# Sums of the MLP's weight blocks by accumulating DMAs, with the last norm in steps between products

## The chip, the cores and the metric

The kernel runs on one core of one Trainium2 chip. A core has engines with instruction queues of their own: TensorE (PE in the profile; PEld is its loading of weights), VectorE (DVE), ScalarE (ACT), GpSimd (POOL) and SyncE (SP), which here only issues DMAs. Each engine takes its instructions in order and waits on semaphores for what others produce. The metric is the device time of one execution in microseconds (us); lower is better. Times given for a kernel are medians of several runs.

## The reference

One layer of a hybrid decoder over 2048 prompt tokens and 32 sample tokens (8 sequences of 4), model width 1024, all in fp32:

```
h = rmsnorm(x, g_mix); proj = h @ w_in            # split into LRU x, LRU gate, SSD z, SSD x/B/C, SSD dt
y_lru = rmsnorm(RG_LRU(conv(lru_x)) * gelu(lru_gate))
y_ssd = rmsnorm(SSD_scan(silu(conv(ssd_xbc)), dt) * silu(ssd_z))
x = x + concat(y_lru, y_ssd) @ w_out              # 2048 -> 1024
h = rmsnorm(x, g_mlp)
x = x + square(relu(h @ w_up)) @ w_down           # 1024 -> 4096 -> 1024
y = rmsnorm(x, g_final)
```

It returns y for both kinds of tokens and the new states of the convolutions, of the LRU and of the SSD.

## The kernel before

**Numbers.** Each fp32 operand is split into a high part rounded to the fast matmul type and a low part (the remainder). A product is three matmuls: high × high, low × high, high × low. For a weight block of a projection `load_w` loads it (`raw`, L210), ACT makes the high part (`wh`, L212) and DVE the remainder (`wl`, L214).

**First phase, 0 to about 1741 us of the profile.** The tokens go through in three parts (768, 640 prompt and 32 sample, 640), each with two token blocks of up to 384. A part runs: the input phase `x_phase` (loads tokens, transposes them, L341, and norms them), `group_front`, eight SSD pairs (`pair_front`, `pair_x`, `pair_mats`, `pair_back`), eight LRU steps (`lru_front`, `lru_back`), then the output projection `proj_add`. That adds three groups of 512 or 1024 rows of `w_out` to the residual tiles `P.X2`: kt = 8 in the middle of the pairs, kt = 12 (half of the SSD's output, operands `n1`) and kt = 0 (the LRU's output, operands `nl`, split by `nl_split` during the kt = 12 call). Each call goes over eight output blocks `o` of 128. kt = 0 was called once for each token block and so loaded and split its eight weight blocks twice. Behind each block stood the square sums, and `residual_out`, which norms the block, and stores the MLP's input to `mn_d` and the residual to `x2_d` in DRAM. The last block's `residual_out` stood behind the next part's `x_phase`.

**Weight blocks of the MLP.** The MLP multiplies 2 × 2 blocks with seven products instead of eight. For each pair of column halves it needs seven matrices made from four weight blocks (some of them sums), split high and low, in `up_d` and `dn_d` in DRAM. Making them is cut into 64 jobs that are strewn through the first phase: `tick` counts work in units (TP at an SSD pair's places, TL at an LRU step's, TO at an output block of the kt = 0 projection) and issues the next stage of the current job each time a unit is full. Before, a job has four stages: load (four DMAs into one tile `jt`, L1077), sums (four DVE adds of 128 × 256, L1082 to L1085, and ACT's rounding into `jh`, L1087), lower (store of `jh`, DVE's remainder in place, L1091) and store (L1094). `jt` and `jh` have one buffer each, so a job's load waits for the job before to be stored.

**Second phase, the MLP.** Three tiles of about 696 tokens, each as two halves of up to 348 columns. For each of eight `q` it runs `up` twice (seven products of 12 matmuls, L816; PSUM from `bank()`) and `down` (four `g`, seven products of six matmuls each). `front` makes the operands of the next tile during the last `q`. `final` is the last norm of the tile before: for each 128 columns it transposes eight blocks of the residual (L975) into two PSUM tiles `fx`, squares and sums on ACT, norms on DVE into `yt` (three buffers, L985) and stores. Before, it was called in one piece behind the two `up` of q = 0, with the loads of the new tile's residual `x2` behind it.

The instructions of every engine's queue are put in order by a scheduler from the dependencies and from the order in which the code is written; nothing is fixed by hand beyond that.

Of the kernel before, what the change touches and what calls it, by code (L numbers as in the profile page):

```python
# [8 lines left out]
F32 = mybir.dt.float32  # L9
# [13 lines left out]
FF = 4096  # L23
# [15 lines left out]
TP, TL, TO = 1.4, 1.6, 1.0  # L39
X2N = ("m", "y", "xdt", "xdd", "hT")  # L40
XTN = ("xdt", "xdd", "hT")
HS, HR = 2, 4
# [3 lines left out]
def hymba_step(ctx: ExitStack, tc: tile.TileContext,  # L46
# [251 lines left out]
    def x_phase(P, mid=None):  # L298
        P.xT = dr.tile([D, P.Lc], F32, name=f"xT{P.i}")
# [28 lines left out]
        early = {}  # L328
        for ti, (a, n, gi) in enumerate(tiles):
            o = P.tt[a][0]  # L330
# [83 lines left out]
    def proj_add(P, src, kt, tiles, bc, blocks=None, hooks={}, tick=None):  # L414

        blocks = range(len(P.blocks)) if blocks is None else blocks
        nk = KD if isinstance(tiles[0], list) else len(tiles)
        per = KD // nk
        for o in range(KD):
            if o in hooks:  # L420
                hooks[o]()
            if tick:
                tick(P, TO)
# [3 lines left out]
            for b in blocks:  # L427
# [362 lines left out]
    def mlp():  # L790
# [11 lines left out]
        def tmp(name):  # L802
            return mp.tile([128, MH], F32, tag="t", name=name, bufs=20)
# [22 lines left out]
        def operands(b, n, tag, bufs):  # L826
# [3 lines left out]
            V.tensor_sub(t1[:, :n], b12[:, :n], b11[:, :n])  # L830
            V.tensor_sub(t2[:, :n], b22[:, :n], t1[:, :n])
            V.tensor_sub(t3[:, :n], b22[:, :n], b12[:, :n])
# [3 lines left out]
        def front(c0, n):  # L836

            out = [[] for _ in range(7)]
            b = []

            def load():
                for k in range(4):
                    b.append([tmp("mb") for _ in range(4)])
                for i in (0, 1, 3, 2):
                    for k in range(4):
                        o, hf = 128 * (k + 4 * (i // 2)), c0 + (i % 2) * n
                        nc.sync.dma_start(b[k][i][:, :n], mn_d[o:o + 128, hf:hf + n])
# [4 lines left out]
            def sub(d, x, y):  # L852
                V.tensor_sub(d[:, :n], x[:, :n], y[:, :n])

            t1 = []

            def one():
                half(0, [x[0] for x in b])
                for x in b:
                    t1.append(tmp("t1"))  # L860
                    sub(t1[-1], x[1], x[0])

            def two():
                for x, t in zip(b, t1):
                    sub(x[0], x[3], t)
                half(1, [x[0] for x in b])
                half(2, t1)

            def three():
                for x in b:  # L870
                    sub(x[1], x[3], x[1])
                half(3, [x[1] for x in b])
                half(4, [x[2] for x in b])
# [413 lines left out]
```

## Time and profile before

| what | value |
|---|---|
| median of three runs | 3186.7 us (3176.54 to 3188.68) |
| profiled execution | 3186.77 us |
| its span in the trace | 3185.0 us |
| mean granted clock of TensorE | 0.949 of full speed |
| busy in the span | PE 92%, PEld 88%, DVE 69%, ACT 44%, POOL 5% |
| DMA | 721.55 MB, q1 (issued by SP) 70.8% of 16 engines' span, q0 (issued by POOL) 0.1% |

A row of a stage table has a stretch of time, its length, the busy us of each engine with its instructions in brackets, the clock that TensorE was granted, the share of the DMA engines and GB/s. A row of groups has the line, engine, operation, tiles, shape and count, then the busy time in all, the mean in ns, the idle time before it and what ended that. A row of waits has who waited for whom, the us in all, how often and the mean.

### The profile page before, as it was taken

The numbers are of one execution on the slowest core, as the hardware profiler recorded it, in microseconds if no ns is written. First come the engines' busy times: TensorE is split into PE (matmuls) and PEld (weight loads), VectorE is DVE, ScalarE is ACT, GpSimd is POOL, SyncE is SP. The second block draws the span as 40 slices with busy tenths as digits, with TensorE's granted clock in tenths as the row PEclk, the third lists the DMA queues.
The fourth block names the chain that finished last, engine by engine and source line by source line (L and its number), as shares of the span: only waits on it lengthen the run. The fifth ranks groups of instructions, "written<-read, shape, count | busy, mean of one in ns | idle before, by whom it ended". The sixth has DMA issues, their size and how long they took to land.

```text
span 3185.0 us, 49175 instructions
## 1 busy us (share of the span) xinstructions
PE 2922.6 (92%) x18150; PEld 2812.0 (88%) x18150; DVE 2207.3 (69%) x4423; ACT 1407.6 (44%) x2580; POOL 158.8 (5%) x270
## 2 busy tenths in 40 slices
PE   7999999899999878998986999999799998699996
PEld 6999998788989877998975899998699998699996
DVE  6888788787777977887886554547555557454546
ACT  5544785444358635545862332324222224222322
POOL 0000110010002100001200000000000000000000
PEclk9999999899999988999997999999899999799997
DMA  6576566866665586565757888888688887688884
GB/s 190 171 227 172 183 195 205 251 187 198 194 187 172 167 268 217 164 207 157 224 171 220 304 270 281 268 284 270 233 274 280 270 283 259 220 269 276 267 279 150
DMA packets 555344, 721.55 MB, mean 227 GB/s; under 512 B 40709, under 2 KB 435129, under 8 KB 555104
## 3 DMA queue, kind: packets, MB, share of 16 engines
q1 hardware_dynamic: 554880, 718.13, 70.8%
q8 instruction: 144, 2.36, 0.3%
q0 software_dynamic: 224, 0.27, 0.1%
q14 instruction: 96, 0.79, 0.1%
HBM read 554.01 MB, written 164.27 MB: 226 GB/s over the span
## 4 chain that ended last, share of the span: by engine, by line
PE 47%; DVE 5%; DMA 5%; ACT 2%; issue 1%; SPq 0%; DVEq 0%; POOL 0%; ACTq 0%
PE mb L816 39%; PE mm L227 2%; PE mm L225 2%; PE mm L226 2%; DMA out_dram<-yt 1%; DMA mb<-mn_d 1%; DMA m<-cum 1%; DMA mw<-up 1%; DVE wl L214 0%; DMA mw<-dn 0%; DMA raw<-in_w_out_dram 0%; DVE yt L985 0%; DVE jt L1091 0%; PE ax L704 0%; DMA dn<-jt 0%
## 5 line engine op out<-in xcount | busy, mean ns | idle before, releaser
L225 PE MATMUL mm<-xh,wh 128*128 128x384 f32 (+3 forms) x2160 | 715.8, 332 | 49.4 <-ACT wh L212 22.0
L227 PE MATMUL mm<-xh,wl 128*128 128x384 f32 (+3 forms) x2160 | 711.9, 331 | 13.4 <-DVE wl L214 13.3
L226 PE MATMUL mm<-xl,wh 128*128 128x384 f32 (+3 forms) x2160 | 710.0, 329 | 1.5 <-DVE xl L360 0.8
L816 PE MATMUL mb<-ahh,mw 128*128 128x346 f32 (+1 forms) x2688 | 659.6, 326 | 18.9 <-DVE nt L242 7.7
L816 PE MATMUL mb<-mhh,mw 128*128 128x346 f32 (+1 forms) x2688 | 650.8, 322 | 25.5 <-DMA mw<-up 25.5
L816 PEld LDWEIGHTS mb<-ahh,mw 128*128 128x128 f32 x2688 | 476.0, 192 | 25.7 <-DVE nt L242 8.7
L816 PEld LDWEIGHTS mb<-mhh,mw 128*128 128x128 f32 x2688 | 475.0, 191 | 26.4 <-issue 21.0
L225 PEld LDWEIGHTS mm<-xh,wh 128*128 128x128 f32 (+1 forms) x2160 | 411.5, 191 | 66.0 <-ACT wh L212 24.9
L816 PE MATMUL mb<-ahl,mw 128*128 128x346 f32 (+1 forms) x1344 | 436.1, 325 | 0.1
L816 PE MATMUL mb<-mhl,mw 128*128 128x346 f32 (+1 forms) x1344 | 436.1, 325 | 0.0
L227 PEld LDWEIGHTS mm<-xh,wl 128*128 128x128 f32 (+1 forms) x2160 | 410.9, 190 | 26.6 <-DVE wl L214 20.4
L226 PEld LDWEIGHTS mm<-xl,wh 128*128 128x128 f32 (+1 forms) x2160 | 411.6, 191 | 7.0 <-DVE xl L360 2.4
L924 DVE TENSOR_TENSOR x<-x,mb 128x346 f32<-128x346 f32 (+1 forms) x480 | 244.3, 514 | 151.5 <-PE mb L816 148.3
L212 ACT ACTIVATE wh<-raw 128x1024 fp32r<-128x1024 f32 (+1 forms) x183 | 190.4, 1042 | 202.6 <-PE mm L226 138.8
L816 PEld LDWEIGHTS mb<-ahl,mw 128*128 128x128 f32 x1344 | 257.9, 192 | 0.6 <-DVE ahl L823 0.6
L816 PEld LDWEIGHTS mb<-mhl,mw 128*128 128x128 f32 x1344 | 254.9, 190 | 0.0
L214 DVE TENSOR_TENSOR wl<-raw,wh 128x1024 fp32r<-128x1024 f32 (+1 forms) x183 | 220.4, 1205 | 43.9 <-ACT wh L212 42.4
L889 ACT ACTIVATE p<-mb 128x346 f32<-128x346 f32 (+1 forms) x48 | 21.8, 455 | 474.9 <-PE mb L816 474.9
L396 DVE SCALAR_TENSOR_TENSOR u<-xe,prm,u 128x768 f32<-128x768 f32 (+2 forms) x180 | 169.7, 943 | 12.6 <-ACT u L394 10.6
L910 ACT ACTIVATE c<-c 128x346 f32<-128x346 f32 (+1 forms) x144 | 71.2, 494 | 203.0 <-DVE c L899 122.9
L823 DVE TENSOR_TENSOR ahl<-c,ahh 128x346 fp32r<-128x346 f32 (+1 forms) x144 | 74.1, 515 | 120.7 <-ACT ahh L822 120.5
L1091 DVE TENSOR_TENSOR jt<-jt,jh 128x1792 fp32r<-128x1792 f32 x64 | 129.3, 2021 | 25.9 <-ACT jh L1087 25.6
(297 smaller groups left out, 4276.1 us busy)
## 6 DMA issues: line engine op xcount, KB each, us to landing
mw<-up SPq DMA_DIRECT2D x336, 512.0 KB
mw<-dn SPq DMA_DIRECT2D x288, 512.0 KB
raw<-in_w_in_dram SPq DMA_DIRECT2D x108, 512.0 KB
raw<-in_w_out_dram SPq DMA_DIRECT2D x72, 512.0 KB
up<-jh SPq DMA_DIRECT2D x32, 896.0 KB
up<-jt SPq DMA_DIRECT2D x32, 896.0 KB
dn<-jh SPq DMA_DIRECT2D x32, 896.0 KB
dn<-jt SPq DMA_DIRECT2D x32, 896.0 KB
```

The lines of the kernel that those rows point to most:

```text
L212: S.activation(h, raw, AF.Copy)
L214: V.tensor_tensor(out=lo, in0=raw, in1=h.bitcast(F32), op=ALU.subtract)
L225: T.matmul(ps[:m, :n], h[:, k, :m], xh[:, c0:c0 + n], start=k == 0, stop=False)
L226: T.matmul(ps[:m, :n], h[:, k, :m], xl[:, c0:c0 + n], start=False, stop=False)
L227: T.matmul(ps[:m, :n], lo[:, k, :m], xh[:, c0:c0 + n], start=False, stop=k == nk - 1)
L396: V.scalar_tensor_tensor(out=u[:, :W], in0=xe[:, k:k + W], scalar=pc(wn, k * nt + j), in1=u[:, :W], op0=ALU.mult, op1=ALU.add)
L816: T.matmul(ps[:, :n], w[:, wi, c], x[:, :n], start=start and k == 0 and i == 0, stop=k == nk - 1 and i == 2, skip_group_check=not start)
L823: V.tensor_sub(lo[:, :n], t[:, :n], h[:, :n].bitcast(F32))
L889: S.activation(p1[:, :n], x[:, :n], AF.Copy)
L910: S.activation(c[:, :n], c[:, :n], AF.Relu)
L924: V.tensor_add(c, c, ps[:, :n])
L1091: V.tensor_tensor(out=jt[j].bitcast(F32R), in0=jt[j], in1=jh[j].bitcast(F32), op=ALU.subtract)
```

## The change

Four pieces go together.

1. The sums of a job are made by DMAs that add to their target, issued by POOL from SBUF to SBUF (`job_add`). The load puts each of the blocks that are needed twice into two places of `jt` at once (source step 0; eight DMAs instead of four, 896 KB instead of 512 KB). As such a DMA can only add, the minus signs move to the other operand and to the places where the products are added up: additions there become subtractions and the reverse, in the same number. A job has seven stages, and TP, TL, TO go from 1.4, 1.6, 1.0 to 2.5, 3.0, 1.0; every `proj_add` ticks now.
2. The projections at a part's end: kt = 12 for o 0 to 3, kt = 0 for both token blocks at once, then kt = 12 for o 4 to 7. `x_phase` is a generator: its pieces for the next part stand at o = 5 of kt = 0 and ahead of each pair of kt = 12 blocks. `residual_out` of both blocks stands behind the next part's `group_front`, in the last part behind everything.
3. `final` gives a list of steps of 128 columns, which `up` takes one by one behind its products 0, 2, 4 and 6 (`FILL`) at q = 0. The last tile's steps use `bank()`. The loads of `x2` stand in `down` at q = 0, two for each `g`.
4. `front` loads 12 of the 16 blocks first and `b21` in its fourth step; the tag `t` has 16 buffers, not 20.

```
-TP, TL, TO = 1.4, 1.6, 1.0
+TP, TL, TO = 2.5, 3.0, 1.0
+FILL = (0, 2, 4, 6)
...
-        for i, at in ((0, (0, 4)), (1, (3, 6))):
+        for at, i, r in ((0, 0, 0), (2, 1, 0), (4, 0, 1), (6, 1, 1)):
             for k in range(2):
-                nc.sync.dma_start(t[:, at[k]].rearrange("p (k n) -> p k n", n=128),
-                                  dap(src, (r0 + dr_ * k) * ld + cols[i], [[ld, 128], [128 * ld, 2], [1, 128]]))
-    def job_sums(j):
-        V.tensor_add(t[:, 2], t[:, 3], t[:, 6])
-        V.tensor_sub(t[:, 3], t[:, 0], t[:, 3])
-        V.tensor_sub(t[:, 1], t[:, 2], t[:, 0])
-        V.tensor_sub(t[:, 5], t[:, 4], t[:, 1])
+                m = min(2, 7 - at)
+                nc.sync.dma_start(t[:, at:at + m, 128 * k:128 * k + 128],
+                                  dap(src, (r0 + dr_ * r + 128 * k) * ld + cols[i], [[ld, 128], [0, m], [1, 128]]))
+    def job_add(j, to, of):
+        nc.gpsimd.dma_start(jt[j][:, to], jt[j][:, of], accum_op=ALU.add)
+    def job_first(j):
+        job_add(j, 2, 6)
+        job_add(j, 3, 0)
+    def job_second(j):
+        job_add(j, 1, 2)
+    def job_third(j):
+        job_add(j, 5, 1)
+    def job_higher(j):
         h = jh[j] = wp.tile([128, 7, 256], F32R, tag="jh", name="jh", bufs=1)
-        S.activation(h, t, AF.Copy)
+        S.activation(h, jt[j], AF.Copy)
...
-stages = (job_load, job_sums, job_lower, job_store)
+stages = (job_load, job_first, job_second, job_third, job_higher, job_lower, job_store)
...
-            V.tensor_add(v[:, :n], p1[:, :n], y[:, :n])
+            V.tensor_sub(v[:, :n], p1[:, :n], y[:, :n])
...
+        proj_add(P, w_out, 12, n1, bc1, range(4), {o: (lambda o=o: hook(o)) for o in range(4)})
+        xn = iter(()) if P.last else x_phase(parts[P.i + 1])
...
-        for b in range(lastb + 1):
-            proj_add(P, w_out, 0, nl, bcl, [b], tick=tick)
-            sums(b)
-            if b < lastb:
-                residual_out(b)
-        carried_out(P)
-        if not P.last:
-            x_phase(parts[P.i + 1])
-        residual_out(lastb)
+        proj_add(P, w_out, 0, nl, bcl, hooks={5: lambda: next(xn, None)})
+        for o in (4, 6):
+            next(xn, None)
+            proj_add(P, w_out, 12, n1, bc1, range(o, o + 2))
+        for _ in xn:
+            pass
+        for b in range(lastb + 1):
+            sums(b)
+        carried_out(P)
...
-                act = [up(q, u, mh, n) for u in range(2)]
-                if prev:
-                    final(*prev)
+                act = [up(q, u, mh, n, fill) for u in range(2)]
```

What this moves is seen in the queues. On PE at the first tile change (`fx` are the transposes of `final`, `mb` the MLP's products) the end of the norm stands before as

```order
L816 MATMUL mb<-ahh,mw 128x346
L975 MATMUL fx<-ident,x_18056 128x128
L975 MATMUL fx<-ident,x_18058 128x128
L975 MATMUL fx<-ident,x_18060 128x128
L975 MATMUL fx<-ident,x_18062 128x128
L975 MATMUL fx<-ident,x_18064 128x128
```

with 32 such rows in a run, four steps of eight. After, the fourth step and what follows it reads

```order
L1000 MATMUL fx<-ident,x_18175 128x128
L822 MATMUL mb<-ahh,mw 128x346
L822 MATMUL mb<-ahl,mw 128x346
L822 MATMUL mb<-ahh,mw 128x346 x2
L822 MATMUL mb<-ahl,mw 128x346
L822 MATMUL mb<-ahh,mw 128x346 x2
```

and some 50 products stand there ahead of the next eight transposes; only the last two steps stand nearly side by side, with five products between them.

On POOL, in the LRU steps of the first part (`xe`, `halo`, `hl` and `u` belong to the LRU; `jt` is the job's tile), the queue before is

```order
L378 COPY xe<-halo 128x3
L770 TENSOR_TENSOR u<-a 128x768
L386 COPY halo<-xe 128x3
L781 COPY hl<-th 128x1
L378 COPY xe<-halo 128x3
```

and after

```order
L1102 DMA jt<-jt 128x256
L776 TENSOR_TENSOR u<-a 128x768
L1102 DMA jt<-jt 128x256 x2
L394 COPY halo<-xe 128x3
L1102 DMA jt<-jt 128x256
L787 COPY hl<-th 128x1
L386 COPY xe<-halo 128x3
```

so the LRU's small work on POOL now stands behind DMAs that wait for a load or for the DMA before.

On PE at the end of part 1 (`mm` with `xh` of 128 columns are projection products, `ax<-ident,xt` the transposes of the next part's tokens, `mm` of 16 columns the next part's first products) the order before is

```order
L227 MATMUL mm<-xh,wl 128x288
L1027 MATMUL ax<-ident,so 24x128 x4
L1027 MATMUL ax<-ident,soh 8x128 x8
L341 MATMUL ax<-ident,xt 128x128 x12
L287 MATMUL nx<-ident,rs 128x128 x3
L341 MATMUL ax<-ident,xt 128x128 x6
L225 MATMUL mm<-xh,wh 16x384
```

and after, where `nh` and `nl` are the operands of kt = 12,

```order
L229 MATMUL mm<-xh,wl 128x288
L349 MATMUL ax<-ident,xt 128x128 x11
L227 MATMUL mm<-nh,wh 128x384
L228 MATMUL mm<-nl,wh 128x384
L229 MATMUL mm<-nh,wl 128x384
L227 MATMUL mm<-nh,wh 128x384
```

so the transposes of the next part's first tokens stand ahead of projection products, and the carried states come behind.

More of the change, by code (lines that the diff above doesn't have):

```diff
@@ L426, in proj_add @@
             w = [t[:, :, 128 * (o % per):128 * (o % per) + 128] for t in ws]
-            for b in blocks:
+            for b in range(len(P.blocks)):
                 c0, n = P.blocks[b]
@@ L849, in half, with sub, loads @@
             def half(op, ts):
                 out[op].extend(halves(t, n, "mh", 56) for t in ts)
-            def sub(d, x, y):
-                V.tensor_sub(d[:, :n], x[:, :n], y[:, :n])
-            t1 = []
+            def sub(d, x, y, op=ALU.subtract):
+                for i in range(4):
+                    V.tensor_tensor(out=d[i][:, :n], in0=x[i][:, :n], in1=y[i][:, :n], op=op)
+            def loads():
+                load(b11, 0, c0)
+                load(b12, 0, c0 + n)
+                load(b22, 512, c0 + n)
@@ L857, in one @@
             def one():
[L858 to L861, printed above, removed]
+                half(0, b11)
+                sub(b11, b11, b12)
             def two():
[L864 to L867, printed above, removed]
+                t2.extend(tmp("t2") for _ in range(4))
+                sub(t2, b22, b11, ALU.add)
@@ L881, in front, with after, up @@
-            return out, [load, one, two, three, four]
-        def up(q, u, mh, n):
+                half(4, b21)
+                half(5, b22)
+                sub(b21, b21, t2)
+                half(6, b21)
+            return out, [loads, one, two, three, four]
+        def after(i, fill):
+            if fill and i in FILL:
+                fill.pop(0)()
+        def up(q, u, mh, n, fill=()):
             src = up_d[2 * q + u]
@@ L887, in up @@
             product(x, weights(src, 0, 512), mh[0], n, True)
+            after(0, fill)
             p1 = tmp("p1")
@@ L903, in up @@
             product(z, weights(src, 5, 512), mh[5], n, False)
+            after(5, fill)
             c12 = tmp("c12")
@@ L968, in final, with step @@
                     m = s1 - c0 - o
+                steps.append((o, m))
+                o += m
+            def step(o, m):
                 ss = sf.tile([128, 8], F32, tag="ssq", name="ssq")
@@ L992, in final @@
                                               yts[hf][lo - c0 - o:hi - c0 - o])
-                o += m
+            return [lambda a=a: step(*a) for a in steps]
         mh, steps = front(*MLP[0])
@@ L1016, in mlp @@
                     steps.pop(0)()
-                down(q, act, x2, us, n, steps)
-            prev = (c0, n, x2)
-        final(*prev)
+                down(q, act, x2, us, c0, n, steps)
+            fill = final(c0, n, x2, i + 1 == len(MLP))
+        for f in fill:
+            f()
     def rows_out(src, j0, nt, m, dst, ld):
@@ L1142, in hymba_step @@
         R0 = group_front(P, 0, lambda: decays(P))
+        if P.i:
+            residual()
         fr = pair_front(P, 0)
```

133 lines of the change are left out of this document (71 added, 62 removed).

## The prediction

> **What bounds the kernel now.** I read the page first: its totals, the tenths of granted clock, the queues. It puts TensorE (PE) at the top and leaves GpSimd (POOL) and its DMA queue all but empty.
>
> ```profile
> span 3185.0 us, 49175 instructions
> PE 2922.6 (92%) x18150; PEld 2812.0 (88%) x18150; DVE 2207.3 (69%) x4423; ACT 1407.6 (44%) x2580; POOL 158.8 (5%) x270
> ...
> q0 software_dynamic: 224, 0.27, 0.1%
> ```
>
> So time can only be had where PE stands still or runs at a lowered clock. A table by stage shows where (columns: stretch, its length, busy us of PE, PEld, DVE, ACT and POOL with counts, granted clock, DMA share, GB/s):
>
> ```profile
> 340.00:500.00 160.00, 152.41 (x859) 150.41 (x858) 134.36 (x173) 133.22 (x176) 29.71 (x29) 0.98 0.59 187
> 500.00:640.00 140.00, 124.53 (x671) 110.80 (x670) 109.90 (x232) 65.96 (x113) 3.33 (x6) 0.89 0.75 233
> 640.00:945.00 305.00, 292.89 (x1951) 268.32 (x1950) 242.38 (x504) 141.98 (x266) 22.78 (x72) 0.96 0.65 189
> ...
> 1090.00:1240.00 150.00, 119.14 (x677) 106.09 (x676) 112.28 (x250) 66.59 (x121) 0.50 (x3) 0.84 0.74 229
> ...
> 1640.00:1760.00 120.00, 80.75 (x468) 75.87 (x467) 83.83 (x174) 37.58 (x58) 2.78 (x1) 0.80 0.69 215
> sum 1720.00, PE 1572.52 PEld 1481.24 DVE 1391.33 ACT 963.89 POOL 156.20; mean PE 174.72 PEld 164.58 DVE 154.59 ACT 107.10 POOL 17.36
> ```
>
> Inside a part (third row: 305 us, the SSD pairs of part 1) PE has 12 us idle and a clock of 0.96. The three boundaries are the bad places: 500–640, 1090–1240 and 1640–1760. In each of them idle time is followed by a lowered clock, so an idle gap is paid more than once. Next the same table for the MLP's products alone (L816; first pair PE, second PEld) at a steady place, at the two tile changes and at the end:
>
> ```profile
> 1820.00:2160.00 340.00, 340.00 (x2137) 339.29 (x2136) 1.00 0.84 276
> 2220.00:2280.00 60.00, 29.67 (x168) 27.68 (x167) 0.74 0.60 198
> 2700.00:2760.00 60.00, 27.76 (x141) 25.76 (x140) 0.69 0.57 185
> ```
>
> The steady MLP is full: 340/2137 = 0.159 us per product. It has nothing to give except at the tile changes. There the transposes of the last norm (L975) wait for one another, and the timeline of PE shows by how much (start, length, work, and in brackets the idle time before it and its releaser):
>
> ```profile
> 2252.47 1.97 PE L975 MATMUL fx<-ident,x 128*128 128x128 f32 x8 [4.00 <-DVE yt L985]
> ...
> 2264.41 1.91 PE L975 MATMUL fx<-ident,x 128*56 128x128 f32 x8 [3.99 <-DVE yt L985]
> 2269.57 0.66 PE L816 MATMUL mb<-ahh,mw 128*128 128x346 f32 x1 [3.25 <-DVE nt L242]
> ```
>
> Each 128-column step costs 2 us of transposes and 4 us of waiting for DVE to empty the two PSUM banks.
>
> **The change part by part.**
>
> *Last norm in steps between products.* In 2220–2280 the products alone would need 168 × 0.159 = 26.7 us, the transposes take 42 × 0.157 = 6.6 us (the row below), so 60 − 26.7 − 6.6 = 26.7 us are lost; in 2700–2760 it is 60 − 141 × 0.159 − 6.6 = 31.0 us.
>
> ```profile
> 2220.00:2280.00 60.00, 9.45 (x42) 6.99 (x42) 0.74 0.60 198
> ```
>
> Together 57.7 us. Now four of the six steps are followed by a product or more of 12 matmuls (1.9 us each at 0.159; the order puts about 45 to 60 of them, 7 to 9 us, behind each), and 4 us of DVE work fit under that. Steps 4 and 5 stand almost side by side and keep one 4.0 us wait; the second wait (3.25 us, for the first operands of `down`) keeps its cause; the small work of the steps now lies between the DVE and ACT work that `up` needs. I leave 11 us lost per change: 57.7 − 22 = 36 gained. Ends: 57.7 if nothing stays, 10 if the evictions of `up` queue behind the six norm steps on DVE and PE waits 4 us at each of the 12 steps (57.7 − 48). The out DMAs of a step move behind up to 12 weight loads on SP's queue and hold `yt` longer; yt has three buffers for two per step, so the next step waits for those DMAs. That is in the 22. The x2 loads move from one run of eight into the four `g` of `down`; the steady stretch has a DMA share of 0.84, so they fit, at 0.
>
> *End of the kernel.* The last six steps have six banks now, but `yt` still has three buffers. The chain of waits there:
>
> ```profile
> 3174.65 0.76 DVE yt L985
> ...
> 3175.43 2.00 DMA out_dram<-yt
> ```
>
> A step's time passes through yt and its store, which the banks don't change: −2 us, between 0 and −6 (one step).
>
> *Order at a part's end.* Against the clock and fill of a quiet stretch (0.97, no idle), 500–640 loses 140 − 124.5 = 15.5 idle and 124.5 × (1 − 0.89/0.97) = 10.3 by clock, 26 us; 1090–1240 loses 30.9 + 16.0 = 47 us. Most of it lies in the next part's input phase, which PE waits for after its last projection product. In the new order that phase runs beside projection products of kt = 0 (o 5 to 7) and kt = 12 (o 4 to 7), and the residual's norm and stores go behind the next part's group_front. Two thirds of 26 + 47 is 48 gained; one third stays, since the square sums and carried_out still stand alone and the residual's DVE work meets the next part. Ends: all 73, and 0 if ACT and DVE, which do both the input phase and the weight splits, only change the order in which they are late. For the third boundary (39 idle, of which the next row shows 20.6) I take 0: there is no next part to overlap, the residual of both blocks now comes in one piece (up to +5), and four of 16 operand loads fewer stand ahead of the first weights (down to −8).
>
> ```profile
> PE mb L816 <- DMA mw<-up: 25.5, 3, 20.6
> ...
> PE mm L227 <- DVE wl L214: 16.9, 21, 1.7
> ...
> PE mm L225 <- DVE x L432: 11.6, 10, 2.3
> ```
>
> *DVE and ACT work taken away.* The sums of the weight blocks are four DVE instructions for each of 64 jobs, and the projections now load and split each kt = 0 weight block once for both token blocks: 24 splits fewer.
>
> ```profile
> L214 DVE TENSOR_TENSOR wl<-raw,wh 128x1024 fp32r<-128x1024 f32 (+1 forms) x183 | 220.4, 1205 | 43.9 <-ACT wh L212 42.4
> ...
> L1085 DVE TENSOR_TENSOR jt<-jt 128x256 f32<-128x256 f32 x64 | 29.8, 466 | 0.8
> ...
> L1083 DVE TENSOR_TENSOR jt<-jt 128x256 f32<-128x256 f32 x64 | 28.0, 437 | 1.0
> ...
> L1082 DVE TENSOR_TENSOR jt<-jt 128x256 f32<-128x256 f32 x64 | 27.2, 425 | 26.2 <-DMA jt<-in_w_up_dram 9.8 <-DMA jt<-in_w_down_dram 8.9 <-issue 7.3
> ...
> L1084 DVE TENSOR_TENSOR jt<-jt 128x256 f32<-128x256 f32 x64 | 26.7, 417 | 0.0
> ```
>
> That is 29.8 + 28.0 + 27.2 + 26.7 = 111.7 us of DVE plus 24 × 1.205 = 29 us of splits. DVE isn't the bound, so it counts only where PE waited for DVE: 16.9 + 11.6 = 28.5 us in the rows above. 141 of the 1391 us of DVE in this phase (the sum row of the table by stage) is a tenth; since DVE's work comes in bursts I take a quarter, −8 us (0 to −28). The signs moved into subtractions cost 0: the same count of DVE operations.
>
> *Sums by accumulating DMAs.* A job now is eight loads, then three dependent links of DMAs of 128 KB on POOL's queue (2+=6 beside 3+=0; 1+=2; 5+=1), then rounding, remainder, two stores. There is one `jt` and one `jh`, so a job's round is a chain; the chain of waits shows one round before:
>
> ```profile
> 1513.61 2.04 DVE jt L1091
> ...
> 1515.66 5.19 DMA dn<-jt
> ...
> 1521.29 0.49 SPq L1077
> ...
> 1521.83 0.46 SPq L1077
> ...
> 1522.34 3.01 DMA jt<-in_w_up_dram
> ...
> 1525.48 0.43 DVE jt L1082
> ...
> 1528.12 1.70 ACT jh L1087
> ```
>
> After: 2.04 + 5.19 + 8 issues × 0.475 + 3.01 + 1.70 + 0.4 of handoffs = 16.1 us, plus 3 L for the links. No accumulating DMA stands in this trace. The nearest rows are POOL's few DMAs:
>
> ```profile
> cum<-cT POOLq DMA_DIRECT2D x1, 48.0 KB, 2.5
> ...
> cum<-cT POOLq DMA_DIRECT2D x1, 40.0 KB, 1.9
> ...
> ecum<-eT POOLq DMA_DIRECT2D x1, 40.0 KB, 6.4
> ```
>
> Ends of L: 1.9 and 6.4 us. I take 2.8: the first row, 2.5, and 0.3 for a transfer some three times as large. So a round is 16.1 + 8.4 = 24.5 us (21.8 to 35.3). By the Trainium skill (DMA: Bandwidth & Descriptors, section on the anatomy of one DMA on the gpsimd path) such a DMA is estimated at 2.0 us + bytes/436e3; 128 KB gives 2.3 us, a round of 23.0 us, and the +20 below would be 0, 3093 us in all. What is free for a round:
>
> ```profile
> sum 1681.00, ACT 106.80; mean ACT 11.87
> ```
>
> That is the rounding instruction (L1087) over 60–1741 us, 64 times: 26.3 us for each job, 25.4 once the boundaries have given 56. A round of 24.5 just fits on the mean, but stages fall at fixed places in the program, and a late link holds the POOL queue (the LRU's copies behind it), then ACT's rounding, then SP's stores with the weight loads behind. I put +20 on it, between 0 (L = 1.9) and 60 + 64 × 35.3 − 1683 = +636 (L = 6.4). The added traffic (about 384 KB more loads for each job, 512 KB of accumulates, less 24 weight blocks of 512 KB) is some 46 MB over 1700 us, 27 GB/s on 190 to 230: at 0, since the DMA share there is 0.6 to 0.75.
>
> **Sum:** −36 − 2 − 48 − 8 + 20 = −74 us. The profiled execution took 3186.77 us (span 3185.0 and 1.8 around it), the median of the three runs is 3186.7, so nothing is to be corrected: 3113 us.
>
> **Rivals.**
> 1. *The chain of jobs becomes the bound of the first 1740 us.* Point of decision: without the +20 the gain is 94, of which 58 lie before the MLP, so the phase ends at 1683; 60 + 64 C = 1683 + 94 gives C = 26.8, L = 3.6. At L = 4.5, C = 29.6 and the end is at 1954, +271: 3187 − 94 + 271 = 3364. For it: one POOL DMA took 6.4, and 190–230 GB/s of other traffic go past. Against: the other rows are 1.9 to 2.5. Nearer the point of decision, L = 4.1, it is 3187 − 94 + (60 + 64 × 28.4 − 1683) = 3288.
> 2. *The boundaries don't close:* ACT and DVE are late as before, 48 becomes about 10: 3151. For it: PE waits there for ACT's and DVE's pieces of the input norm, both of which now also serve products. Against: DVE is at 110 of 140 and ACT at 66 of 140 in that stretch.
> 3. *The norm between the products stalls them* (the 10 end above, evictions and SP's queue): 3113 + 26 = 3139.
> 4. *POOL is held by DVE.* POOL's own small copies show it: the same copy of 128x3 takes from 0.18 to 2.9 us.
>
> ```profile
> L378 POOL COPY xe<-halo x60: 176/186/2885, 36.7 to 1592.9; 128x3 f32<-128x3 f32 x60
> L386 POOL COPY halo<-xe x60: 185/527/1995, 53.8 to 1599.0; 128x3 f32<-128x3 f32 x60
> ```
>
> If each link pays the usual excess (0.527 − 0.185 = 0.34 us), C is 25.5, and the jobs cost some 10 us more than forecast, 3123; if each pays the worst (2.7 us), C is 32.6, and 60 + 64 × 32.6 − 1683 = +463. I hold the first for the likely form, with a quarter of the chance at a middle of 1 us (C = 27.5, +137, 3230). The Trainium skill (SBUF — State Buffer, the box on DVE blocking DMAs) says that a DMA issued from GpSimd can't write its descriptors while DVE holds their shared port in a fast copy, and looks blocked: it speaks against this change, and the spread of the copies agrees that DVE can hold POOL, but no row here shows a DMA held.
>
> **How the numbers follow.** Forecast 3113: 0.46. Rival 1: 0.20. Rival 2: 0.14. Rival 3: 0.12. Rival 4: 0.08. A measurement of this kernel can tell 0.5% from no change, 16 us: below 3171 or above 3203. Faster: 0.45 of the forecast, 0.11 of rival 2, 0.10 of rival 3, 0.05 of rival 4, 0.71. Slower: 0.17 of rival 1, 0.02 of rival 4, 0.01 of rival 2, 0.20. Same: the remaining 0.09. The range goes from 3060 (the good ends of half the terms: 3113 − 20 − 25 − 8) to 3250, inside rival 1 (L = 3.6 gives 3187, L = 3.9 gives 60 + 64 × 27.8 − 1683 = +156, 3249); 0.06 lies below and 0.12 above. The forecast's own range is 3075 to 3150.
>
> **What would show it.** Right: q0 carries some 33 MB, and an accumulate lands in about 3 us; a round of the job chain is 24 to 25 us; the MLP begins near 1705; the two tile changes have some 11 us lost each, and no run of eight transposes waits 4 us except one; the clock at 500–640 and 1090–1240 goes above 0.92. Wrong: an accumulate of 4 us or more, ACT's rounding or POOL's copies waiting for it, SP's issues waiting for ACT; idle stretches at the boundaries as before with other releasers; products released by the evictions of `up` at the tile changes. The prediction fails above all on L, and next on the share of the boundary that closes.

## The result, and the profile after

| | before | changed |
|---|---|---|
| median | 3184.8 us (4 runs, 3176.5 to 3188.7) | 3377.1 us (4 runs, 3374.4 to 3381.7) |
| ratio to before | 1 | 1.061 (95% interval 1.058 to 1.063) |
| span of the profiled execution | 3185.0 us | 3373.8 us |
| first product of the MLP | 1756.8 us | 1986.4 us |
| from there to the end | 1428.2 us | 1387.4 us |

The forecast was 3113 us; the change is 6.1% slower. The MLP became 41 us shorter and the first phase 230 us longer. The time of run 6 below leaves out one execution that took 5932.7 us. The first phase is read from the start of the MLP's first product (rows of before and of the changed kernel; ns shortest, median, longest, then first and last start in us):

```profile
L816 PE MATMUL mb<-mhh,mw x2688: 317/322/629, 1756.8 to 3119.2; 128*128 128x346 f32 x128, 128*128 128x348 f32 x64
```

```profile
L822 PE MATMUL mb<-mhh,mw x2688: 315/322/628, 1986.4 to 3307.8; 128*128 128x346 f32 x128, 128*128 128x348 f32 x64
```

The page of the changed kernel, against the rows shown of before:

```profile
span 3373.8 us, 50181 instructions
PE 2964.2 (88%) x18150; PEld 2849.1 (84%) x18150; DVE 2096.8 (62%) x4143; ACT 1383.1 (41%) x2556; POOL 363.0 (11%) x526
...
q0 software_dynamic: 37088, 33.85, 6.8%
...
jt<-jt POOLq DMA_DIRECT2D x256, 128.0 KB, 3.4
```

DVE is busy for 110 us less, and q0 carries the 33 MB of accumulates. Yet PE's share fell: 1946 us of first phase for the same work as before in 1716 (the first row is of before, up to its first MLP product, the second of the changed kernel; columns as in the table by stage).

```profile
40.00:1756.00 1716.00, 1569.34 (x9860) 1478.03 (x9858) 1389.61 (x2536) 963.89 (x1551) 156.20 (x258) 0.95 0.65 197
```

```profile
40.00:1986.00 1946.00, 1624.36 (x9858) 1529.71 (x9857) 1278.99 (x2251) 939.00 (x1525) 360.39 (x514) 0.90 0.72 197
```

PE's idle time grew from 147 to 322 us, and its granted clock fell from 0.95 to 0.90, with 55 us more busy time for the same products. The waits (who waited for whom, us in all, times, longest) name the jobs:

```profile
POOL jt L1102 <- DMA jt<-jt: 357.0, 112, 7.2
...
DVE jt L1120 <- ACT jh L1116: 265.0, 53, 12.9
...
ACT jh L1116 <- DMA jt<-jt: 195.1, 32, 18.3
...
PE mm L227 <- ACT xe L391: 54.5, 16, 7.3
PE mm L227 <- DVE x L438: 53.4, 15, 11.0
```

The rows of before that belong to the third, second and fourth of these (the fifth, L432, stands in the prediction):

```profile
ACT jh L1087 <- DVE jt L1085: 68.4, 24, 7.1
...
DVE jt L1091 <- ACT jh L1087: 25.6, 29, 3.1
...
PE mm L225 <- ACT xe L383: 11.5, 8, 3.7
```

Read from the top: POOL waits for one accumulating DMA before it can issue the next; ACT's rounding (L1116) waits for the last; DVE's remainder (L1120) waits for ACT, ten times as long as before; and PE waits 54.5 and 53.4 us, before 11.5 and 11.6, for other work of ACT and DVE, which take their queues in order. A round of one job can be followed in the timeline, here on POOL:

```profile
1130.03 0.88 POOL L1102 DMA_DIRECT2D jt<-jt  x1 [2.46 <-issue]
1131.22 0.86 POOL L1102 DMA_DIRECT2D jt<-jt  x1 [0.31 <-issue]
...
1137.51 0.86 POOL L1102 DMA_DIRECT2D jt<-jt  x1 [4.46 <-DMA jt<-jt]
...
1140.49 0.86 POOL L1102 DMA_DIRECT2D jt<-jt  x1 [0.87 <-DMA jt<-jt]
```

and on ACT, DVE and SP behind it:

```profile
1145.17 1.70 ACT L1116 ACTIVATE jh<-jt 128x1792 fp32r<-128x1792 f32 x1 [5.58 <-issue]
...
1146.90 2.03 DVE L1120 TENSOR_TENSOR jt<-jt,jh 128x1792 fp32r<-128x1792 f32 x1 [6.06 <-ACT jh L1116]
...
1148.96 0.56 SPq L1123 DMA_DIRECT2D up<-jt  x1
1154.06 3.92 SPq L1098 DMA_DIRECT2D jt<-in_w_down_dram  x8
```

From the first accumulating DMA to the rounding 15 us pass. SP holds the next load until the store has landed, as there is one `jt`; it waited for that in 52 rounds (in before in 38):

```profile
SPq L1098 <- DMA up<-jt: 88.2, 28, 6.9
...
SPq L1098 <- DMA dn<-jt: 63.8, 24, 5.6
```

Over the 63 rounds the starts in the timeline give these medians (us): rounding to remainder 1.7, remainder to store 2.1, store to the next load 5.7, the eight loads' issues 4.0, to the first DMA 0.9, to the second 1.6, to the third 4.9, to the fourth 3.2, to the next rounding 2.9. Their sum is 26.9 us (27.0 from the rounded figures), of which 12.5 us stand for the links. This is a middle and no floor: 8 of the 63 rounds were shorter, the shortest 24.5 us. The rounds themselves, from the starts of the rounding, look so:

| rounds (us) | mean | quartiles | shortest |
|---|---|---|---|
| before | 26.1 | 19.1, 22.7, 29.9 | 16.0 |
| changed | 30.1 | 27.8, 29.5, 31.3 | 24.5 |

The ends of the two series of 64 roundings are these rows (first and last start):

```profile
L1087 ACT ACTIVATE jh<-jt x64: 1680/1697/1721, 51.6 to 1695.1; 128x1792 fp32r<-128x1792 f32 x64
```

```profile
L1116 ACT ACTIVATE jh<-jt x64: 1687/1701/1711, 64.3 to 1959.6; 128x1792 fp32r<-128x1792 f32 x64
```

Before, half of the rounds took less than 23 us, and three over 50. In the changed kernel there are hardly any short rounds, and the last rounding stands 27 us ahead of the MLP instead of 62. The theory to be tested is the *theory of the rounds*: each round lasts the longer of the chain and of what the program puts between two jobs. If the n rounds of a kernel whose chain doesn't bind are filled up to a chain of C, the first phase grows by the sum of (C − round) over the shorter ones. The rivals: the accumulates' *traffic*; and a *queue theory* or *theory of standing*, in which the waits of POOL, ACT and DVE at a job's stages cost by themselves, however much room a round has.

The MLP did what was forecast. Its products alone, in 140 us around each tile change, before and changed:

```profile
2160.00:2300.00 140.00, 101.81 (x601) 98.02 (x600) 0.87 0.74 249
...
2640.00:2780.00 140.00, 99.19 (x554) 95.65 (x554) 0.83 0.70 236
```

```profile
2390.00:2530.00 140.00, 117.21 (x692) 111.70 (x691) 0.95 0.83 276
...
2870.00:3010.00 140.00, 123.00 (x734) 118.38 (x734) 0.96 0.84 278
```

At 0.159 us for a product, 91 and 180 more of them in the same time are 14.5 and 28.6 us, 43 in all.

### The profile page after: what moved, and what is told of

It reads as the page before. It is cut to its first block, busy times and chain, and to the rows that moved or that the text cites. A ratio compares the mean times of both kernels' runs of the same rounds, so it can differ in the third digit from the quotient of the medians.

```text
span 3373.8 us, 50181 instructions
## 1 busy us (share of the span) xinstructions
PE 2964.2 (88%) x18150; PEld 2849.1 (84%) x18150; DVE 2096.8 (62%) x4143; ACT 1383.1 (41%) x2556; POOL 363.0 (11%) x526
## 5 line engine op out<-in xcount | busy, mean ns | idle before, releaser
L227 PE MATMUL mm<-xh,wh 128*128 128x384 f32 (+3 forms) x2160 | 726.2, 337 | 95.2 <-ACT xe L391 54.5
L228 PE MATMUL mm<-xl,wh 128*128 128x384 f32 (+3 forms) x2160 | 719.7, 334 | 1.1 <-DVE xl L481 1.0
L227 PEld LDWEIGHTS mm<-xh,wh 128*128 128x128 f32 (+1 forms) x2160 | 420.5, 195 | 114.7 <-ACT xe L391 60.1
L229 PEld LDWEIGHTS mm<-xh,wl 128*128 128x128 f32 (+1 forms) x2160 | 418.5, 194 | 20.1 <-DVE wl L216 13.8
L228 PEld LDWEIGHTS mm<-xl,wh 128*128 128x128 f32 (+1 forms) x2160 | 419.6, 194 | 7.1 <-DVE xl L481 2.2
L1102 POOL DMA_DIRECT2D jt<-jt x256 | 221.5, 867 | 1025.6 <-DMA jt<-jt 357.0
L1120 DVE TENSOR_TENSOR jt<-jt,jh 128x1792 fp32r<-128x1792 f32 x64 | 129.5, 2024 | 267.1 <-ACT jh L1116 265.0
L214 ACT ACTIVATE wh<-raw 128x1024 fp32r<-128x1024 f32 (+1 forms) x159 | 165.5, 1042 | 220.0 <-PE mm L228 205.4
L1116 ACT ACTIVATE jh<-jt 128x1792 fp32r<-128x1792 f32 x64 | 108.8, 1701 | 340.3 <-DMA jt<-jt 195.1
L216 DVE TENSOR_TENSOR wl<-raw,wh 128x1024 fp32r<-128x1024 f32 (+1 forms) x159 | 191.1, 1202 | 33.0 <-ACT wh L214 32.0
```

Source lines behind the costliest of these rows:

```text
L214: S.activation(h, raw, AF.Copy)
L216: V.tensor_tensor(out=lo, in0=raw, in1=h.bitcast(F32), op=ALU.subtract)
L227: T.matmul(ps[:m, :n], h[:, k, :m], xh[:, c0:c0 + n], start=k == 0, stop=False)
L228: T.matmul(ps[:m, :n], h[:, k, :m], xl[:, c0:c0 + n], start=False, stop=False)
L229: T.matmul(ps[:m, :n], lo[:, k, :m], xh[:, c0:c0 + n], start=False, stop=k == nk - 1)
L1102: nc.gpsimd.dma_start(jt[j][:, to], jt[j][:, of], accum_op=ALU.add)
```

## The experiments

Each is an edit of the changed kernel unless it says otherwise; times are medians, each against the kernel before on the same chip (medians 3183 to 3197 us).

**1. Sums by DVE at the same places.**

```
-        nc.gpsimd.dma_start(jt[j][:, to], jt[j][:, of], accum_op=ALU.add)
+        V.tensor_add(jt[j][:, to], jt[j][:, to], jt[j][:, of])
```

> The changed kernel with one thing undone: the four sums of a job are DVE adds again (four of 128 x 256), at the same places of the program, with the same eight loads, seven stages and ticks; the projections' order and the norm's steps stay. Chain theory (the round of one job, load to load, paces the first phase; in the changed kernel it takes 30.1 us on the mean, of which 14.1 us lie in the links of the accumulating DMAs): the links fall to about 4 x 0.45 + handoffs = 3 us, the round to some 19 us, below what the program offers, and the phase is as long as its other work: the MLP starts near 1700 to 1730 us, the time is 3090 to 3120 us. Queue theory (the stages' places in the in-order queues cost, whoever adds): half of the 230 us stays, 3200 to 3260 us. Traffic theory (the added DMA bytes cost): 256 DMAs gone, the larger loads stay; 3110 to 3150 us.

Measured: 3130.8 us, ratio 0.982 (0.980 to 0.984); the MLP begins at 1739.1. Who adds is worth 247 us of first phase (1986.4 − 1739.1). 3131 lies just above the chain's range and inside the traffic's, so this run alone does not tell the two apart; runs 2 and 3 bear on that, and run 7 shows where the excess is.

**2. One link instead of three, same DMAs.**

```
-        job_add(j, 1, 2)
+        job_add(j, 1, 4)
...
-        job_add(j, 5, 1)
+        job_add(j, 5, 4)
```

> The changed kernel with the same 256 accumulating DMAs and bytes, but the second and third read a block that the load has brought (1+=4 and 5+=4 in place of 1+=2 and 5+=1), so none waits for another: one link in a row instead of three (the sums are other ones). Chain theory: 5.0 + 3.9 us of waiting between links become about 1.3 us of issue each, the round falls from 30.1 to some 24 us, the time to 3110 to 3170 us. Traffic theory: nothing changes, 3360 to 3390 us. Queue theory: ACT and DVE wait at the same places but shorter, 3200 to 3300 us.

Measured: 3264.3 us, ratio 1.024 (1.020 to 1.027); MLP at 1870.3. Bytes and count being the same, 116 us came back, so traffic alone is not the cause. But 131 us over run 1 stayed, more than the chain alone would give, and this run doesn't say what they are. The four DMAs in flight together took longer each (median 4.4 us to landing, not 3.4).

**3. One link more.**

```
         job_add(j, 5, 1)
+        job_add(j, 5, 1)
```

> The changed kernel with the last accumulating DMA done three times in place of once... in fact twice: job_third issues 5+=1 two times (another sum), so a job has four dependent links instead of three and 320 DMAs instead of 256. Chain theory: one more link of 3.4 to 5 us in each of 64 rounds, +220 to +320 us, 3600 to 3700 us, the MLP's length unchanged at 1387 us. Traffic theory: a quarter more of the accumulates' traffic, +50 us at most, 3430 us. Queue theory: between, 3450 to 3500 us.

Measured: 3528.7 us; MLP at 2139.3, +153, with the MLP itself unchanged. The mean round went from 30.1 to 32.6 us. My +220 took each round to grow by a whole link; the mean grew by 2.5 us, less than a link, so I read it that rounds with room took the rest in. A quarter more DMAs would, by traffic alone, have cost a quarter of 247 us, 62. By the rounds (chain 30.2) the phase should be 434 us over run 1; it is 400.

**4. Only the jobs changed, in the kernel before.** (Its MLP's output has other signs.)

```
-TP, TL, TO = 1.4, 1.6, 1.0
+TP, TL, TO = 2.5, 3.0, 1.5
...
-    stages = (job_load, job_sums, job_lower, job_store)
+    stages = (job_load, job_first, job_second, job_third, job_higher, job_lower, job_store)
```

> The kernel before with the jobs of the changed one alone (eight loads, accumulating DMAs, seven stages; ticks 2.5, 3.0, 1.5, as its kt = 0 ticks at 16 places of a part and not at 24); projections, norm and the signs in the products stay as before, so its MLP output has other signs. Chain theory: the first phase grows to about 60 + 64 x 30 = 1980 us, whatever its order, the MLP keeps its 1428 us: 3400 to 3440 us. If the order of the projections is what costs, it stays at 3187 to 3250 us.

Measured: 3452.9 us, ratio 1.083 (1.080 to 1.086); MLP at 2027.6, +271 over before. So the changed jobs alone bring the loss, without the new order; the run takes their eight loads, seven stages and ticks over together with the accumulating DMAs, which run 1 separates. Filling the rounds of before up to 26.9 us gives +262.

**5 and 6. Half of the jobs, by DMA and by DVE.**

```
-TP, TL, TO = 2.5, 3.0, 1.0
+TP, TL, TO = 1.25, 1.5, 0.5
...
-            src = up_d[2 * q + u]
+            src = up_d[2 * (q - q % 2) + u]
...
-    for q in range(NQ):
+    for q in range(0, NQ, 2):
```

> The changed kernel with 32 of the 64 jobs (those of every second q; the MLP of the other q's reads the matrices of the q before) and ticks of half the size, so that a job gets about 50 us of the program in place of 25; each job is as before, with its accumulating DMAs. Theory of the rounds (a round lasts the longer of the chain, 27 to 30 us, and of what the program puts between the same stage of two jobs; where the chain is longer, the engines stand): almost no round is short any more, so it comes within 30 us of the same kernel with DVE's sums. Queue theory (each stage costs by standing in an in-order queue, whatever the pace): half of the 247 us stays, 110 to 130 us more than with DVE's sums. Traffic theory: half as well.

> The control of the run with half of the jobs: the same 32 jobs, places and ticks, with the four sums as DVE adds. All theories: a little below the kernel with DVE's sums and all jobs (3131), as DVE, ACT and the DMAs have half the job work: 3085 to 3125 us.

Measured: 3164.7 us by DMA (MLP at 1769.1) and 3070.2 by DVE (1676.6; a single execution, the profiled one, span 3068.5). The MLP starts 92 us apart, and not under 30. My expectation failed on its premise: the rounds weren't 50 us long. The jobs were drawn forward in the order of the queues: in run 6 the last of 32 was rounded at 990 us, the mean round was 30.2 us, and 16 of 31 were shorter than 26.9. Filled up to 26.9 us, the rounds of run 6 give 69 of the 92 us. So the run speaks for the rounds no more than for the queues.

**7. The job as before (four loads, four DVE sums, four stages), all else changed.**

```
-TP, TL, TO = 2.5, 3.0, 1.0
+TP, TL, TO = 1.4, 1.6, 0.7
...
-        for at, i, r in ((0, 0, 0), (2, 1, 0), (4, 0, 1), (6, 1, 1)):
+        for i, at in ((0, (0, 4)), (1, (3, 6))):
...
+        V.tensor_add(t[:, 2], t[:, 3], t[:, 6])
+        V.tensor_add(t[:, 3], t[:, 3], t[:, 0])
+        V.tensor_add(t[:, 1], t[:, 0], t[:, 2])
+        V.tensor_add(t[:, 5], t[:, 4], t[:, 1])
```

> The changed kernel with the job as it was before (four loads, four DVE sums with the new signs and ACT's rounding in one stage, four stages, ticks 1.4, 1.6 and 0.7); projections' order and norm's steps as changed. If the seven stages and the eight loads cost something in the kernel with DVE's sums, it is faster than 3131: 3095 to 3125 us. If not, 3125 to 3140 us, and then the new order at the parts' ends brought only about 18 us of the 48 + 8 forecast.

Measured: 3098.5 us, ratio 0.972 (0.970 to 0.974); MLP at 1707.6. The eight loads and seven stages, with their ticks, cost 32 us in run 1. The new order at the parts' ends, with 24 splits fewer, is worth 1756.8 − 1707.6 = 49 us of the two traces, 44 by the medians of runs 8 and 7.

**8. Only the MLP changed, in the kernel before.** The diff is the MLP's part of the change, with additions in the DVE sums.

> The kernel before with the changed MLP alone (norm in steps between products, loads of x2 and of the first blocks moved, signs in the products, with additions in the DVE sums to match); first phase as before. The forecast had -36 for the tile changes and -2 for the end, the MLP of the changed kernel is 41 us shorter in its trace: 3140 to 3155 us. If the MLP's gain needed the other parts: over 3165 us.

Measured: 3142.3 us, ratio 0.986 (0.984 to 0.988), −44.5 us by the medians. With run 7: −44.5 − 43.9 = −88.4.

**9. Two empty stages ahead of the rounding.**

```
-TP, TL, TO = 2.5, 3.0, 1.0
+TP, TL, TO = 3.2, 3.9, 1.3
...
-    stages = (job_load, job_first, job_second, job_third, job_higher, job_lower, job_store)
+    stages = (job_load, job_first, job_second, job_third, job_gap, job_gap, job_higher, job_lower, job_store)
```

> The changed kernel with two empty stages between the last accumulating DMA and ACT's rounding (nine stages, ticks 3.2, 3.9 and 1.3, so that the jobs keep their pace). Theory of the rounds (what counts is the longer of the chain, 27 us, and of the program's time between two jobs): the chain and the number of jobs are the same, 3350 to 3400 us. Queue theory (ACT and DVE stand because the rounding is put too near behind the links): ACT's waits for the links mostly go, 3230 to 3300 us.

Measured: 3391.6 us, ratio 1.064 (1.061 to 1.067): no gain. The waits are nearly the same as in the changed kernel:

```profile
DVE jt L1123 <- ACT jh L1119: 258.8, 56, 13.0
...
ACT jh L1119 <- DMA jt<-jt: 185.4, 31, 14.4
```

This is as expected by the rounds; but since the waits hardly changed, the gap hardly moved the rounding, so the queue theory was not put to the test.

**10. The best version, with six buffers of `yt`.** (Kernel of run 7.)

```
-                    yt = mp.tile([128, 512], F32, tag="yt", name="yt", bufs=3)
+                    yt = mp.tile([128, 512], F32, tag="yt", name="yt", bufs=6)
```

> The best version so far (changed order and norm, jobs with DVE's sums in four stages, 3098 us, ratio 0.972) with six buffers of yt in place of three. At the end a step of the last norm takes 6.0 us, of which 2.0 are the store of yt on which the next step's yt waits: with six buffers a step should take some 3 to 4 us, five steps 10 to 15 us less, and the waits of the transposes at the tile changes shrink by a few us: 3080 to 3090 us, ratio 0.966 to 0.970. If the steps at the end are bound by DVE and ACT alone, no change: 3098.

Measured: 3066.1 us, ratio 0.962 (0.960 to 0.964). The norm's transposes' waits for `yt` fall from

```profile
PE mb L1000 <- DVE yt L1010: 10.7, 3, 4.1
PE fx L1000 <- DVE yt L1010: 10.0, 5, 3.8
```

in run 7 to

```profile
PE mb L1000 <- DVE yt L1010: 4.3, 3, 2.5
...
PE fx L1000 <- DVE yt L1010: 1.3, 5, 0.3
```

From the last MLP product to the end it is 23 us instead of 39, and from the first product to the last 1338 instead of 1351. I had the end right (10 to 15 us expected, 16 measured) and the tile changes too small (13 us). It is the fastest version of this study.

**11. Only the two independent sums by DMA.**

```
-        job_add(j, 1, 2)
+        V.tensor_add(jt[j][:, 1], jt[j][:, 1], jt[j][:, 2])
...
-        job_add(j, 5, 1)
+        V.tensor_add(jt[j][:, 5], jt[j][:, 5], jt[j][:, 1])
```

> The changed kernel with only the first two sums of a job by accumulating DMAs (2+=6 and 3+=0, which don't wait for one another) and the other two as DVE adds; places, loads and ticks as changed. Theory of the rounds: the chain falls from 26.9 us (sum of the medians of its steps in the changed kernel) by the second link, 4.9, and the third, 3.2, and gains two DVE adds with handoffs, 1.2: about 20 us. Of the rounds of the kernel with DVE's sums (3131) 23 of 63 are shorter than 20.1 us, and filling these up costs 24 us: 3140 to 3170 us. Queue theory (a link costs 247/256 us by standing there): half of the 247 us, 3240 to 3270 us.

Measured: 3232.3 us, ratio 1.013 (1.004 to 1.021); MLP at 1836.6, +97 over run 1 where the rounds allow 24. The theory of the rounds misses here. DVE's first add stands in its queue for the DMA:

```profile
DVE jt L1109 <- DMA jt<-jt: 133.8, 41, 7.1
```

These are 41 waits of 3.3 us on the mean. I read it so that a stage put right behind a slow one costs, although its round has room; no run shows that apart from the rest, and the time lies a little under the queue theory's range too.

**12. Plain copies in place of accumulating DMAs.** (The matrices are overwritten, not added to.)

```
-        nc.gpsimd.dma_start(jt[j][:, to], jt[j][:, of], accum_op=ALU.add)
+        nc.gpsimd.dma_start(jt[j][:, to], jt[j][:, of])
```

> The changed kernel with its 256 DMAs on the same queue, of the same size and in the same dependences, as plain copies: they overwrite their target in place of adding to it, so the weight matrices are other ones. If it is the adding that makes a link long, the landing falls well under the 3.4 us of the changed kernel, towards 2.5, the chain to some 24 us and the time to 3250 to 3320 us. If it is the queue and the traffic, landing and time stay: 3.3 to 3.5 us, 3360 to 3390 us.

Measured: 3265.6 us; MLP at 1874.7, 112 us earlier than with adding. POOL's issue takes less time (first row changed, second this run; ns shortest, median, longest):

```profile
L1102 POOL DMA_DIRECT2D jt<-jt x256: 836/862/1425, 46.0 to 1956.6; - x128
```

```profile
L1102 POOL DMA_DIRECT2D jt<-jt x256: 536/538/582, 46.6 to 1844.5; - x128
```

and the landing 3.0 us instead of 3.4. The medians of the links fall to 1.6, 4.1, 2.8 and 2.3, the chain to 25.2 us.

**13 and 14. The remainder on POOL, then the rounding too.** DVE, then DVE and ACT, have no part in a job's end.

```
-        V.tensor_tensor(out=jt[j].bitcast(F32R), in0=jt[j], in1=jh[j].bitcast(F32), op=ALU.subtract)
+        G.tensor_tensor(out=jt[j].bitcast(F32R), in0=jt[j], in1=jh[j].bitcast(F32), op=ALU.subtract)
```

(and in run 14 `G.tensor_copy(h, jt[j])` for ACT's rounding)

> The changed kernel with a job's remainder (the subtraction of 128 x 1792) on POOL in place of DVE; accumulating DMAs, ACT's rounding, stages and ticks as changed. DVE then never stands for a job, but the chain grows by what POOL is slower (about 3.2 us for 2.0, from the LRU's product on POOL, 1.34 us for 128 x 696). Theory of the rounds: 28 us and more, 3390 to 3440 us. Theory of standing (DVE's idle time ahead of the jobs' instructions, 265 us, is what costs): most of the 247 us comes back, ACT's waits of some 195 us stay and cost a part: 3150 to 3260 us.

> The changed kernel with rounding and remainder of a job on POOL: the jobs then run on POOL's and SP's queues alone. The chain is some 3 us longer (3.2 + 3.2 in place of 1.7 + 2.0). Theory of the rounds: about 30 us on all 64, 3420 to 3480 us. Theory of standing: neither ACT nor DVE waits for a job, and they have 238 us less work; the first phase comes to 1700 us or less, unless SP's queue (weight loads behind a job's stores) takes over: 3080 to 3160 us.

Measured: 3489.9 us, ratio 1.096 (1.092 to 1.100), and 3455.6 us, 1.085 (1.081 to 1.088); MLP at 2094.6 and 2067.4. DVE's 265 us of standing for the rounding are gone, and the kernel is slower. POOL needs 4.0 us for the remainder where DVE needs 2.0, and the mean round went from 30.1 to 31.9 us, about what the chain got longer:

```profile
L1116 ACT ACTIVATE jh<-jt x64: 1687/1699/1711, 62.4 to 2071.4; 128x1792 fp32r<-128x1792 f32 x64
L1120 POOL TENSOR_TENSOR jt<-jt,jh x64: 3949/4012/5483, 64.2 to 2073.2; 128x1792 fp32r<-128x1792 f32 x64
```

So the loss doesn't hang on DVE's standing alone. Two things blur it: the chain got longer by 2 us in each round, and DVE's own instructions got slower beside POOL's (the split of a weight block took 1449 ns on the mean and not 1202; last section).

**15. The best version with the job on POOL, no accumulating DMA.** (Sums, rounding and remainder of run 10 as POOL instructions.)

```
+        G.tensor_add(t[:, 2], t[:, 3], t[:, 6])
...
-        S.activation(h, jt[j], AF.Copy)
+        G.tensor_copy(h, t)
...
-        V.tensor_tensor(out=jt[j].bitcast(F32R), in0=jt[j], in1=jh[j].bitcast(F32), op=ALU.subtract)
+        G.tensor_tensor(out=jt[j].bitcast(F32R), in0=jt[j], in1=jh[j].bitcast(F32), op=ALU.subtract)
```

> The best version (changed order and norm, four stages, six buffers of yt, 3066 us) with a job's sums, rounding and remainder as POOL instructions: no accumulating DMA, no work for ACT and DVE. DVE loses 4 x 0.42 + 2.02 us and ACT 1.70 us in each of 64 jobs, 237 + 109 us. If their queues are what TensorE waits for in the first phase, 3020 to 3055 us. If POOL's work slows DVE's (both go to the same memory) or the jobs get too slow on POOL, 3065 to 3150 us.

Measured: 3324.7 us, ratio 1.045 (1.041 to 1.048); MLP at 1962.7, although the last job was rounded at 1633.6. That is 270 us over the good end and 175 over the bad one, and not by the chain, whose last round ended 25 us later than in run 10. POOL is busy for 797 us instead of 160, and DVE's instructions are slowed (last section). How the 253 us by which the MLP starts later than in run 10 divide between these two is open.

**The runs together.** What the rounds give, against the first phase measured over run 1 (of run 4 over before, of run 5 over run 6):

| run | chain C (us) | by the rounds | measured |
|---|---|---|---|
| 11 two sums by DMA | 20.1 | 24 | 97 |
| 2 one link | 22 | 68 | 131 |
| 12 plain copies | 25.2 | 186 | 136 |
| 5 half of the jobs | 26.9 | 69 | 92 |
| changed | 26.9 | 261 | 247 |
| 4 jobs alone | 26.9 | 262 | 271 |
| 9 two empty stages | 27.2 | 275 | 253 |
| 14 remainder and rounding on POOL | 28.6 | 349 | 328 |
| 13 remainder on POOL | 28.9 | 364 | 356 |
| 3 one link more | 30.2 | 434 | 400 |

C is the sum of the medians of the steps of that run's own rounds (of the changed kernel's for runs 4 and 5), so the table checks sizes and foretells none. For run 11 C is the estimate that its expectation gives, and for run 2 the 5% quantile of its rounds; with the medians of their own rounds (22.9 and 22.4 us) run 11 would be given 101 us and run 2 84. Where the chain binds in few rounds such medians hold room of the program too, and no run shows which C is right there.

Where C is some 27 us or more and all jobs run, filling the rounds gives the loss within 35 us. Even this is looser than it looks: in the changed kernel the 63 rounds grew by 311 us over run 1 and not by 261, while the time from the last rounding to the MLP shrank from 100 to 27 us. Elsewhere filling gives 50 us too much for run 12 and 23 to 73 us too little for runs 5, 2 and 11; run 11's wait row shows standing there.

Shown is: the adding by DMA is 247 us of loss (run 1), and the changed jobs bring it into the kernel before as well (4). With the same DMAs and bytes, two dependences fewer bring 116 us back (2); one more adding DMA at the end of the chain costs 153 (3), far more than its share of the traffic. Longer chains cost more (13, 14), and more places in the program don't help (9). That the loss goes by the rounds fits these sizes, but is in part argued. Left open is what the 131 us that stay in run 2 are made of, and a kernel with two jobs in flight, that is with a second `jt`, was not run.

## Why the prediction was wrong, point by point

- *Bound and stages.* Right: boundaries and tile changes were where time could be had.
- *Last norm in steps, −36, and the end, −2.* Right: −41 in the trace, −44.5 alone by the medians (run 8). By the sums over 140 us, 22 and 16 us stayed lost at the tile changes beside the transposes, where I said 11; but in this wider stretch 37 and 44 us were lost before, and not 27 and 31. So the gain was right, and both levels were too low.
- *Order at a part's end, −48, and fewer splits, part of −8.* Right in size, 49 us (run 7), and Rival 2 falls. That the size is so near is in part luck: run 7 was only about 8 us ahead of before behind the first boundary (its 4200th matmul, transposes counted, began at 743 us against 751), where my terms have 17, and about 41 behind the second (the 8400th at 1419 against 1460), so 33 there for my 31, and the rest came at the third, for which I took nothing.
- *Sums off DVE.* The rest of the −8 can't be seen: DVE was busy for 110 us less, and no run separates what PE gained by it.
- *Accumulating DMAs, +20.* This is the step that failed. Against run 7, which has all of the change but the new jobs, it came out at 1986.4 − 1707.6 = 279 us: 247 for the adding by DMA and 32 for the loads, stages and ticks (run 1). All other terms together gave 3093 us, and run 7 took 3098.5. The step failed in two places. First L: I took 2.8 us for a link from one plain DMA of POOL, of 48 KB. A link in the chain took 3.2 to 4.9 us from issue to issue and 2.9 to the rounding, the second issue 1.6 more. The links took 12.5 us in all where I had 8.4, the other steps 14.4 where I had 16.1, so the chain was 26.9 and not 24.5 us. An adding DMA takes POOL 0.86 us to issue where a plain one takes 0.54 (run 12). By the fit in the Trainium skill (DMA: Bandwidth & Descriptors, the anatomy of one DMA on the gpsimd path) the estimate for 128 KB is 2.3 us. Here the shortest adding DMA took 2.6 us to land and the median one 3.4 (plain copies in run 12: 1.9 and 3.0), so that estimate would have misled further.
- Second, and larger: "a round of 24.5 just fits on the mean". The mean round of before was 26.1 us, but 35 of 63 rounds were shorter than 24.5 us, and time left in a long round doesn't help a short one, since there is one `jt`. With my own C, filling up the rounds of before gives +170 us, not +20, and the forecast would have been 3187 − 94 + 170, some 3260; with the measured chain of 26.9 us it gives +262. This estimate rests on the theory of the rounds, which fits the runs at these lengths of the chain. The distribution stood in the trace of before; I read only its sum row.
- *Rival 1* was the right one, with 0.20. Its point of decision, L = 3.6 or C = 26.8, was worked out on the mean too; by filling up the rounds of before it lies near C = 22, where 88 us of the 94 are gone. Its prices also stayed below what came: by its sum the measured 12.5 us of links give C = 28.6 and some 3300 us.
- *Rival 4.* No row shows DVE holding POOL's DMAs: their issues took 0.84 us at best, 0.86 on the median and 1.43 at worst. That doesn't exclude it for the landings, which spread from 2.6 to 9.9 us. *Rival 3* falls with run 8.

## What to carry to other kernels

A chain that goes through one buffer must be compared with each gap in which it has to run, not with the mean gap: list the rounds, fill up the short ones, and add. That is an estimate; here it came within 35 us where the chain was long, and not where it was short. Work that is moved off an engine which isn't waited for gains little, and pays the new latency once for each dependent step; here 112 us of DVE work that PE hardly waited for became three links of 3 to 5 us in each of 64 jobs. A change of several pieces is worth taking apart: the other three pieces were worth 88 us without the accumulating DMAs (run 7), and with three more buffers of `yt` 120 us, 3.8% under before.

## What the runs showed of the hardware

An accumulating DMA of 128 x 256 fp32 within SBUF took 0.86 us of POOL and 3.4 us to land (2.6 at best), a plain copy of the same shape 0.54 and 3.0 us (runs of the changed kernel and 12). And beside POOL's elementwise work some of DVE's instructions take much longer: the split of a weight block, two inputs of 128 x 1024, in run 10 and in run 15,

```profile
L216 DVE TENSOR_TENSOR wl<-raw,wh 128x1024 fp32r<-128x1024 f32 (+1 forms) x159 | 190.8, 1200 | 11.8 <-ACT wh L214 10.6
```

```profile
L216 DVE TENSOR_TENSOR wl<-raw,wh 128x1024 fp32r<-128x1024 f32 (+1 forms) x159 | 243.5, 1532 | 41.1 <-ACT wh L214 39.4
```

is 28% longer on the mean, while POOL's DMAs left it at 1202 ns in the changed kernel. It is not slower throughout. The same instructions' shortest, median and longest times in run 10 and in run 15 are

```profile
L216 DVE TENSOR_TENSOR wl<-raw,wh x159: 273/1218/1229, 28.8 to 1660.5; 128x1024 fp32r<-128x1024 f32 x156, 128x128 fp32r<-128x128 f32 x3
```

```profile
L216 DVE TENSOR_TENSOR wl<-raw,wh x159: 282/1224/5101, 28.6 to 1912.8; 128x1024 fp32r<-128x1024 f32 x156, 128x128 fp32r<-128x128 f32 x3
```

Of the 156 of 128 x 1024 in run 15, the 78 that ran while no instruction of POOL did took 1.23 us at most, and the other 78 1.89 us on the mean, up to 5.10. The Trainium skill (SBUF — State Buffer, section on who interferes with whom) says that a DVE instruction with two inputs in SBUF contends with a GpSimd instruction that reads SBUF; the rows agree.
